# Sparse attention's projections in a two-layer fp32 decoder: seven raw weight buffers instead of three, compressions yielded in four parts, scales and second weights moved to the weights' DMA queue

## The chip, the cores and the metric

One core of one Trainium2 chip runs the whole program, in one launch. The metric is the device time of that launch in microseconds. The core has five engines with their own instruction streams: PE (TensorE, the matrix products), ACT (ScalarE), DVE (VectorE), POOL (GpSimd) and SP (SyncE, which here issues DMAs). They meet by semaphores. An engine executes its stream in order: where one instruction waits, all behind it on that engine wait too.

## The reference

A decoder trunk on x of 1 x 256 x 1024 in fp32, two layers. Layer 0 mixes tokens with native sparse attention (NSA), layer 1 with forgetting attention (FoX); behind each stands an MLP with a squared ReLU.

```python
def reference(x, norm_g, mlp_w_up, mlp_w_down, nsa_w_in, nsa_cmp_pos, nsa_cmp_w1, nsa_cmp_w2, nsa_w_out, ...):
    for i in range(DEPTH):                      # 2
        h = rms_norm(x, norm_g[i, 0])
        m = nsa_mixer(h, ...) if kind == 0 else fox_mixer(h, ...)
        x = x + rms_norm(m, norm_g[i, 1])
        h = rms_norm(x, norm_g[i, 2])
        x = x + rms_norm(squared_relu_mlp(h, mlp_w_up[i], mlp_w_down[i]), norm_g[i, 3])

def nsa_mixer(h, w_in, cmp_pos, cmp_w1, cmp_w2, w_out, cos, sin):
    proj = h @ w_in                             # q, kc, vc, ks, vs, kw, vw, gate
    kcmp = nsa_compress(kc_t, cmp_pos[0], cmp_w1[0], cmp_w2[0])   # silu(windows @ w1) @ w2
    vcmp = nsa_compress(vc_t, cmp_pos[1], cmp_w1[1], cmp_w2[1])
    ...                                         # compressed, selected and windowed branch, gated
    return o.reshape(B, T, H * dh) @ w_out
```

The compression takes 15 overlapping windows of 32 tokens, flattens each (2048 numbers for each of 4 groups), and puts it through a small MLP with 256 hidden units.

## The kernel before, in words

**Products in three.** fp32 operands are split into a rounded part `hi` and the rest `lo`, both in a reduced fp32 type. A product of two fp32 matrices is three products on PE: hi by hi, lo by hi, hi by lo (`mm3`, lines 158 to 160). Tokens stand as two tiles of 128.

**Weights.** Each weight comes in chunks of 128 x 1024 numbers (512 KB). `load_w` (lines 120 to 137) takes a buffer `raw`, issues the DMA from SP (line 131), and splits it: ACT copies `hi` (line 117), DVE subtracts to get `lo` (line 118). A `raw` buffer is free again when its `lo` is done, a `hi`/`lo` pair when PE has used it. The main pool `wpool` has three `raw` and six pairs. Two smaller pools with one `raw` and two pairs each come later: `xpool`, when the evacuation buffers `ev` are closed in the middle of the attention, and `ypool`, when the whole of the attention is done. `load_w` goes round all pools that exist.

**Order of the work.** The string `PLAN` lists the steps of NSA: `c` (blocks that feed the compressions), `v`, `k`, `q` (projection blocks of 256 columns), `p0` and `p1` (the two compressions), and, for the attention, `C`, `S`, `V`, `T` (compressed branch, scores, values, transposes of the output). Each `c`, `v`, `k`, `q`, `p` is a generator; a mention advances it to its next `yield`. `|` closes the compressions' pool; `/` closes `ev` and opens `xpool`. A scheduler then sets each engine's order from dependences and buffers; `keep_in_program_order` pins single instructions to the written order.

**Compression.** `compress` (around lines 428 to 490) builds windows, multiplies them by `w1` in four chunks (line 448) without a `yield` between, adds the halves to `hid` (line 452), transposes it (line 456), applies a sigmoid (line 461) and multiplies by the second weights `w2` (lines 469 and 483). `w2` is loaded by two DMAs of 128 KB from ACT's queue at the start of the program.

**Steps the prediction names.** `q_evac` turns a finished q block into `qr` with rotary embedding (lines 247 to 250), splits it to `qs` and transposes it (line 390) for the scores. `k_evac` and `c_evac` do the like with `kk` (lines 357, 358, 367) and `kd` (lines 336, 344). In the attention, scores are exponentiated on ACT (line 572), transposed on PE (line 585), copied on ACT (`pts`, line 587), and multiplied with the values (line 590); POOL adds the branches (lines 594, 595); PE transposes the result (line 601), and ACT and DVE split it to `aT` (shown as `hT`).

**What follows.** `out_proj` multiplies `aT` by `w_out` in eight chunks p0 to p7 of 128 rows; token tile 0 sums into `ps_m`, tile 1 into `ps_o`, 512 columns each: 96 products. `add_norm` applies the scale g[0][1], `mlp` begins with the scale g[0][2]. Each scale is a 512 KB broadcast load (`load_g`, lines 111 to 114) from ACT's queue.

Of the kernel before, what the change touches and what calls it, by code (L numbers as in the profile page):

```python
# [8 lines left out]
F32 = mybir.dt.float32  # L9
# [4 lines left out]
P = 128  # L14
D = 1024
# [27 lines left out]

PLAN = ("c0 v0 v0 v0 c0 c0 v0 p0 c1 c1 c1 c1 k0 k0 k0 c1 c1 k0 p0 p1 k1 k0 k1 p0 k1 k0 k1 p0 v1 v1 k1 v1 k1 v1 "
# [3 lines left out]
SB_B = 4  # L50
# [6 lines left out]
LEAD = 6  # L57
# [13 lines left out]
def kernel(ctx, tc, x_in, norm_g, w_up, w_down, nsa_w_in, nsa_pos, nsa_w1, nsa_w2,  # L71
                             nsa_w_out, fox_w_in, fox_b_f, fox_w_out, consts, out):
    nc = tc.nc
# [5 lines left out]
    hpool = ctx.enter_context(tc.tile_pool(name="hpool", bufs=2))  # L79
# [6 lines left out]
    def ps_tile(use):  # L86
        return psum.tile([P, 512], F32, name="ps_" + use)
# [20 lines left out]
    cmask = cst[:, C_CMASK:C_CMASK + NT * 16].rearrange("p (t c) -> p t c", t=NT)  # L108
    rowv = cst[:, C_RV:C_RV + NT]
    caus = cst[:, C_CAUS:C_CAUS + P]  # L110
    def load_g(layer, j):
        g = hpool.tile([P, D], F32, name="gb")
        nc.scalar.dma_start(g, norm_g[layer, j:j + 1, :].broadcast_to([P, D]))
        return g

    def split(hi, lo, src):
        act.copy(hi, src)  # L117
        dve.tensor_tensor(out=lo, in0=src, in1=hi.bitcast(F32), op=OP.subtract)  # L118

    def load_w(src, nk, n, later=None):  # L120

        wtiles.append(wtiles.pop(0))
        pool_, nraw = wtiles[-1]

        def view(a):
            return a[:, :nk * n].rearrange("p (k n) -> p k n", k=nk)

        raw = view(pool_.tile([P, 1024], F32, name="raw", bufs=nraw))
        hi = view(pool_.tile([P, 1024], R, name="hi"))
        lo = view(pool_.tile([P, 1024], R, name="lo"))  # L130
        nc.sync.dma_start(raw, src)
        if later is None:
            split(hi, lo, raw)
        else:
            later.append(lambda: act.copy(hi, raw))
            later.append(lambda: dve.tensor_tensor(out=lo, in0=raw, in1=hi.bitcast(F32), op=OP.subtract))
        return hi, lo
# [14 lines left out]
    def queue(ins):  # L152
        if as_traced[0]:
            tc.keep_in_program_order(ins)
# [22 lines left out]
    def new_hT():  # L177

        both = hpool.tile([P, 2, KD, T], R, name="hT")
        return both[:, 0], both[:, 1], both  # L180
# [45 lines left out]
    def tok(hT, k, t):  # L226
        s = slice(t * P, (t + 1) * P)
        return hT[0][:, k, s], hT[1][:, k, s]
# [36 lines left out]
        nc.sync.dma_start(xs[1][:, js], x_in[0, P:T, js])  # L265
    nc.sync.dma_start(cst, consts[:, 0:C_ID])
    hT = new_hT()
    ps = ps_tile("t")
    pe.transpose(ps[:, 0:KD], g8, ident[0:KD, 0:KD])
    dve.tensor_copy(gcol, ps[:, 0:KD])  # L270
# [50 lines left out]
    w2 = cp.tile([P, 2, 2, 2, DH], F32, name="w2")  # L321
    pos_sb = hpool.tile([CLEN // 2, 2, P], F32, name="pos_sb", tag="gb")
    nc.scalar.dma_start(pos_sb, nsa_pos[0].rearrange("j (l two) d -> l j (two d)", two=2))
    for dup in range(2):
        nc.scalar.dma_start(w2[:, :, :, dup, :], nsa_w2[0].rearrange("j (k p) d -> p j k d", p=P))
    ps = ps_tile("t")
    for j in range(2):
        pe.transpose(ps[:, j * 16:(j + 1) * 16], pos_sb[:, j, :], ident[0:16, 0:16])
# [100 lines left out]
    def compress(j):  # L429
# [5 lines left out]
        src = bass.AP(base.tensor, base.offset, [base.ap[0], [2, 16], base.ap[1], [CSTR, NC_]])  # L435
# [7 lines left out]
        for k in range(0, 16, 4):  # L443
            w1 = load_w(wr[:, k:k + 4, :], 4, CH)
            for i in range(4):
                lhs = win2[:, k + i].rearrange("p u c -> p (u c)")
                for u in range(2):
                    queue(pe.matmul(ps[:, 0:CH], lhs, w1[u][:, i, :], start=(k + i + u == 0), stop=(k + i + u == 16)))
        hid = cp.tile([NW, CH], F32, name="hid")
        hs = cp.tile([NW, CH], F32, name="hs")  # L450
        act.copy(hs, ps[64:64 + NW, 0:CH])
# [145 lines left out]
    def attn_T(t, p0, n, on):  # L597

        pt = ps_tile("t")
        for j in range(n):  # L600
            pe.transpose(pt[:, j * P:(j + 1) * P], on[:, 2 * j:2 * j + 2, :].rearrange("p h d -> p (h d)"), ident)
        s = slice(t * P, (t + 1) * P)
        split(aT[0][:, p0:p0 + n, s], aT[1][:, p0:p0 + n, s], pt[:, 0:n * P].rearrange("p (n q) -> p n q", n=n))
# [8 lines left out]
    env, scores, oc, on = {}, {}, {}, {}  # L612
    for cmd in PLAN.split():
        op, arg = cmd[0], cmd[1:]
        if cmd in gens:
            if cmd not in env:
                env[cmd] = gens[cmd]()
            next(env[cmd], None)
            as_traced[0] |= cmd == "c0"
        elif op == ";":  # L620
            as_traced[0] = False
        elif op == "|":
            cmp_ctx.close()
            at = nsa_ctx.enter_context(tc.tile_pool(name="at", bufs=2))
            aT = new_hT()
        elif op == "/":
            ev_ctx.close()
            xpool = ctx.enter_context(tc.tile_pool(name="xpool", bufs=NX_HI, side="right"))
            wtiles += [(xpool, NX_RAW)] * NX_HI
        else:  # L630
            t, p = int(arg[0]), int(arg[1])
            if op == "C":
                oc[t, p] = cmp_attn(t, p)
            elif op == "S":
                scores[t, p] = pair_s(t, p)
            elif op == "V":
                if p % AG == 0:
                    on[t, p // AG] = at.tile([P, 2 * AG, DH], F32, name="on")
                i = 2 * (p % AG)
                pair_v(t, p, scores.pop((t, p)), oc[t, 2 * p // HB], on[t, p // AG][:, i:i + 2, :])  # L640
            elif op == "T":
                attn_T(t, AG * p, AG, on[t, p])
# [43 lines left out]
        finish(rest or ())  # L686
        finish(done(1) or ())

    def out_proj(src, w, layer, after, lead=0):

        g = load_g(layer, 1)
        acc = [lambda c=c: [ps_tile(c) for _ in range(2)] for c in "mo"]
        steps = [(lambda p=p: load_w(w[p * P:(p + 1) * P, :].unsqueeze(1), 1, D), lambda t, p=p: tok(src, p, t))
                 for p in range(KD)]

        def done(t):
            add_norm(t, acc[t], g)
            return after[0](t)

        yield from accumulate(acc, steps, done, lead)  # L700


    def mlp(layer, projection, prepare, after):

        mctx = ExitStack()
        mp = mctx.enter_context(tc.tile_pool(name="mlp", bufs=2))
        g = load_g(layer, 2)
        hT = new_hT()
        qs = []

# [11 lines left out]
        prepare.append(prep)  # L722
        finish(projection)
        g3 = load_g(layer, 3)
        NB = DFF // BW
        us = {}
# [89 lines left out]
        return gen  # L816

    prepare = []
    mlp(0, out_proj(aT, nsa_w_out[0], 0, prepare), prepare, to_fox)


    fox_ctx = ExitStack()
# [2 lines left out]
    hT = fox_in["hT"]  # L825
# [67 lines left out]
    aT = new_hT()  # L893
# [87 lines left out]
            cumsum()  # L981

    prepare = []
    projection = out_proj(aT, fox_w_out[0], 1, prepare, LEAD)

    def fill(n):
        for _ in range(n):
# [15 lines left out]

    fox_ctx.close()

    mlp(1, projection, prepare, None)


# [50 lines left out]
```

## Time and profile before

| | |
|---|---|
| time, median of 3 runs | 677.07 us (673.74 to 677.78) |
| the profiled execution's own time | 679.41 us |
| its span in the profile | 677.6 us |
| PE busy | 655.0 us, 97% of the span |
| ACT busy, DVE busy | 375.3 us (55%), 446.4 us (66%) |
| moved by DMA | 110.17 MB, mean 163 GB/s |
| mean granted clock of PE | 0.99 |

Times in the profile count from the span's start. The projections lie up to about 112 us, with the last compression's end at 83 us; the attention proper runs to about 163 us; `out_proj`'s remaining products to 179.4 us, where the first product of the MLP's `up` starts. "Busy" counts every instruction from start to end; products on PE overlap, so the pitch from start to start is shorter than the duration shown. The page shows 40 equal slices; a table of windows shows the same for stretches that one chooses. Waits are told as "engine, output, line, what released it: total us, times, longest".

### The profile page before, as it was taken

Reading aid. Unit: us, or ns where it says so; the run is one execution under the profiler, and the core shown is the slowest. Engines: PE = TensorE matmul, PEld = TensorE weight load, DVE = VectorE, ACT = ScalarE, POOL = GpSimd, SP = SyncE. Lnnn points to the kernel's source line nnn. Section 1 sums busy time; section 2 is a strip of 40 time slices with the busy share of each in tenths; the row PEclk is TensorE's granted clock in tenths of the full one; section 3 lists DMA queues with packets and bytes.
Section 4 is the critical chain, followed back from the end, with each engine's and each line's share of the span. In section 5 each row is a group of like instructions: output and inputs, shape, how many; then the busy total and the mean of one; then the engine's idle time right before and its main releaser. Section 6 shows DMA issues by size and latency. Waiting matters only on the chain.

```text
span 677.6 us, 10581 instructions
## 1 busy us (share of the span) xinstructions
PE 655.0 (97%) x3993; PEld 571.0 (84%) x3993; DVE 446.4 (66%) x854; ACT 375.3 (55%) x654; POOL 38.5 (6%) x77
## 2 busy tenths in 40 slices
PE   8899999999999999999999989999989999999996
PEld 7888898988888888888889979887878888888884
DVE  4777787754985746566649666774967475566533
ACT  4786677755874545445437655664665345455421
POOL 1000002322100000000005000000100000000000
PEclk9999899999999999999999998999989999999998
DMA  9666743201687646656545853442566566465301
GB/s 308 199 168 202 229 130 124 64 1 34 213 290 218 212 154 215 206 167 211 166 126 148 257 173 108 125 125 64 184 188 194 160 211 211 144 209 184 117 1 62
DMA packets 74802, 110.17 MB, mean 163 GB/s; under 512 B 4696, under 2 KB 60672, under 8 KB 74752
## 3 DMA queue, kind: packets, MB, share of 16 engines
q1 hardware_dynamic: 72336, 105.48, 50.2%
q10 hardware_dynamic: 2416, 4.03, 1.8%
q8 instruction: 31, 0.51, 0.3%
q14 instruction: 19, 0.16, 0.1%
HBM read 108.44 MB, written 1.05 MB: 162 GB/s over the span
## 4 chain that ended last, share of the span: by engine, by line
PE 76%; DMA 9%; DVE 6%; ACT 5%; issue 2%; POOL 1%; SPq 0%; POOLq 0%; DVEq 0%; ACTq 0%
PE ps_m L750 13%; PE ps_m L751 8%; PE ps_o L158 5%; PE ps_o L159 5%; PE ps_o L160 5%; DMA raw<-in_nsa_w_in_dram 5%; PE ps_s L160 5%; PE ps_s L158 5%; PE ps_s L159 5%; PE ps_m L158 4%; PE ps_m L159 4%; PE ps_m L160 4%; PE ps_o L590 3%; ACT hi L117 3%; DVE lo L118 3%; DMA raw<-in_fox_w_in_dram 3%
## 5 line engine op out<-in xcount | busy, mean ns | idle before, releaser
L118 DVE TENSOR_TENSOR lo<-raw,hi 128x1024 fp32r<-128x1024 f32 (+2 forms) x196 | 236.8, 1213 | 127.5 <-ACT hi L117 125.4
L117 ACT CAST hi<-raw 128x1024 fp32r<-128x1024 f32 (+2 forms) x196 | 203.4, 1044 | 144.7 <-DMA raw<-in_mlp_w_up_dram 42.2
L750 PE MATMUL ps_m<-hT,hi 128*128 128x512 f32 x392 | 140.1, 396 | 0.0
L751 PE MATMUL ps_m<-hT,lo 128*128 128x256 f32 x448 | 116.6, 280 | 0.0
L751 PEld LDWEIGHTS ps_m<-hT,lo 128*128 128x128 f32 x448 | 84.5, 189 | 5.0
L750 PEld LDWEIGHTS ps_m<-hT,hi 128*128 128x128 f32 x392 | 73.6, 188 | 16.2
L158 PE MATMUL ps_m<-hi,hT 128*128 128x256 f32 (+3 forms) x236 | 77.1, 327 | 1.9 <-ACT hT L117 1.9
L159 PE MATMUL ps_m<-hi,hT 128*128 128x256 f32 (+3 forms) x236 | 75.9, 321 | 1.6 <-DVE hT L118 1.6
L160 PE MATMUL ps_m<-lo,hT 128*128 128x256 f32 (+3 forms) x236 | 75.4, 320 | 0.0
L160 PE MATMUL ps_s<-lo,uh 128*128 128x512 f32 x128 | 50.5, 395 | 0.0
L159 PE MATMUL ps_o<-hi,ul 128*128 128x512 f32 x128 | 50.5, 395 | 0.0
L158 PE MATMUL ps_s<-hi,uh 128*128 128x512 f32 x128 | 50.5, 395 | 0.0
L158 PE MATMUL ps_o<-hi,uh 128*128 128x512 f32 x128 | 50.5, 395 | 0.0
L159 PE MATMUL ps_s<-hi,ul 128*128 128x512 f32 x128 | 50.5, 394 | 0.0
L160 PE MATMUL ps_o<-lo,uh 128*128 128x512 f32 x128 | 50.4, 394 | 0.0
L158 PEld LDWEIGHTS ps_m<-hi,hT 128*128 128x128 f32 x236 | 45.6, 193 | 5.4 <-ACT hT L117 2.4
L159 PEld LDWEIGHTS ps_m<-hi,hT 128*128 128x128 f32 x236 | 45.7, 194 | 4.6 <-DVE hT L118 2.5
L160 PEld LDWEIGHTS ps_m<-lo,hT 128*128 128x128 f32 x236 | 45.7, 194 | 2.4
L755 ACT COPY second<-ps_m 128x256 f32<-128x256 f32 x56 | 20.8, 371 | 38.7 <-PE ps_m L753 38.7
L158 PE MATMUL ps_m<-hT,hi 128*128 128x256 f32 x128 | 38.5, 301 | 0.0
L159 PE MATMUL ps_m<-hT,lo 128*128 128x256 f32 x128 | 36.5, 286 | 0.0
L160 PE MATMUL ps_m<-hT,hi 128*128 128x256 f32 x128 | 36.5, 285 | 0.0
(242 smaller groups left out, 1119.8 us busy)
## 6 DMA issues: line engine op xcount, KB each, us to landing
raw<-in_mlp_w_up_dram SPq DMA_DIRECT2D x64, 512.0 KB, 3.9
raw<-in_mlp_w_down_dram SPq DMA_DIRECT2D x64, 512.0 KB, 4.2
raw<-in_fox_w_in_dram SPq DMA_DIRECT2D x22, 512.0 KB, 4.6
raw<-in_nsa_w_in_dram SPq DMA_DIRECT2D x18, 512.0 KB, 4.6
raw<-in_nsa_cmp_w_dram SPq DMA_DIRECT2D x8, 512.0 KB, 4.1
raw<-in_nsa_w_out_dram SPq DMA_DIRECT2D x8, 512.0 KB, 4.1
raw<-in_fox_w_out_dram SPq DMA_DIRECT2D x8, 512.0 KB, 3.5
gb<-in_norm_g_dram ACTq DMA_DIRECT2D x7, 512.0 KB, 6.0
```

The lines of the kernel that those rows point to most:

```text
L117: act.copy(hi, src)
L118: dve.tensor_tensor(out=lo, in0=src, in1=hi.bitcast(F32), op=OP.subtract)
L158: queue(pe.matmul(ps, lhs[0], rhs[0], start=start, stop=False))
L159: queue(pe.matmul(ps, lhs[1], rhs[0], start=False, stop=False))
L160: queue(pe.matmul(ps, lhs[0], rhs[1], start=False, stop=stop))
L590: pe.matmul(pov[:, hh, br, :], pts[:, j * P:(j + 1) * P], vt[:, kt, br, g, :], start=(kt == 0), stop=(kt == t))
L750: pe.matmul(psv, wh[:, fs], hT[2][:, :, k, :], start=k == 0, stop=False)
L751: pe.matmul(psv[:, 0, :], wl[:, fs], hT[0][:, k, :], start=False, stop=False)
L755: act.copy(second, psv[:, 1, :])
```

## The change

1. **Seven raw buffers.** A tile `other` of four chunks is put into the second buffer of the pool's `hT` tag, and `load_w` takes its raw buffer in turn from `other` and from `wpool`: four and three, seven in all. At `|`, where the attention takes that buffer for `aT`, the list is set back and `load_w` uses three again.
2. **Compressions in four parts.** `compress` yields after each of the first three chunks of `w1`, and `PLAN` is rewritten up to the first scores: quarters of `p0` and `p1` stand between halves of projection blocks.
3. **Second weights.** The two `w2` loads leave ACT's queue at the start and are pinned on SP's queue behind the first `w1` load.
4. **Scales.** g[0][1] and g[0][2] leave ACT's queue and are issued on SP's, pinned, at `/`; the next weight's DMA is pinned behind them (`behind`). `out_proj` and `mlp` get the scale as an argument.

```diff
-PLAN = ("c0 v0 v0 v0 c0 c0 v0 p0 c1 c1 c1 c1 k0 k0 k0 c1 c1 k0 p0 p1 k1 k0 k1 p0 k1 k0 k1 p0 v1 v1 k1 v1 k1 v1 "
+PLAN = ("c0 v0 v0 v0 c0 c0 v0 p0 c1 c1 c1 c1 p0 k0 k0 p0 k0 c1 c1 k0 p0 k1 k1 p0 p1 k1 k0 k0 k1 v1 p0 v1 p1 k1 v1 "
...
     def load_g(layer, j):
         g = hpool.tile([P, D], F32, name="gb")
-        nc.scalar.dma_start(g, norm_g[layer, j:j + 1, :].broadcast_to([P, D]))
+        src = norm_g[layer, j:j + 1, :].broadcast_to([P, D])
+        if layer == 0 and j < 3:
+            tc.keep_in_program_order(nc.sync.dma_start(g, src))
+            behind[0] = True
+        else:
+            nc.scalar.dma_start(g, src)
         return g
...
+    spare = [None]
+
     def load_w(src, nk, n, later=None):
...
-        raw = view(pool_.tile([P, 1024], F32, name="raw", bufs=nraw))
+        spare.append(spare.pop(0))
+        raw = view(spare[-1] if spare[-1] is not None else pool_.tile([P, 1024], F32, name="raw", bufs=nraw))
         hi = view(pool_.tile([P, 1024], R, name="hi"))
         lo = view(pool_.tile([P, 1024], R, name="lo"))
-        nc.sync.dma_start(raw, src)
+        i = nc.sync.dma_start(raw, src)
+        if behind[0]:
+            tc.keep_in_program_order(i)
+        behind[0] = False
...
     hT = new_hT()
+    other = hpool.tile([P, 4, 1024], F32, name="other", tag="hT")
+    spare[:] = [other[:, 0], None, other[:, 1], None, other[:, 2], None, other[:, 3]]
...
-    for dup in range(2):
-        nc.scalar.dma_start(w2[:, :, :, dup, :], nsa_w2[0].rearrange("j (k p) d -> p j k d", p=P))
...
+            if k == j == 0:
+                for dup in range(2):
+                    tc.keep_in_program_order(
+                        nc.sync.dma_start(w2[:, :, :, dup, :], nsa_w2[0].rearrange("j (k p) d -> p j k d", p=P)))
+                behind[0] = True
+            if k < 12:
+                yield
...
         elif op == "|":
             cmp_ctx.close()
+            spare[:] = [None]
...
         elif op == "/":
             ev_ctx.close()
+            scale01, scale02 = load_g(0, 1), load_g(0, 2)
             xpool = ctx.enter_context(tc.tile_pool(name="xpool", bufs=NX_HI, side="right"))
...
-    mlp(0, out_proj(aT, nsa_w_out[0], 0, prepare), prepare, to_fox)
+    mlp(0, out_proj(aT, nsa_w_out[0], scale01, prepare), scale02, prepare, to_fox)
```

The lines of code shift by up to 20 in the changed kernel: the split is at lines 124 and 125 there, the weights' DMA at 141, the products at 171 to 173, the copies `pts` at 607, the output's transposes at 621.

The order of instructions moves at three places that matter below.

**SP, from the last load of the projections on.** `raw_1245` is the last q chunk. Before, chunks p0 to p5 of `w_out` follow at once (`raw_2085` to `raw_2161`), into `wpool`:

```order
L131 DMA raw_1245<-in_nsa_w_in_dram 128x4x256
L131 DMA raw_2085<-in_nsa_w_out_dram 128x1024
L131 DMA raw_2107<-in_nsa_w_out_dram 128x1024
L131 DMA raw_2125<-in_nsa_w_out_dram 128x1024
L131 DMA raw_2137<-in_nsa_w_out_dram 128x1024
L131 DMA raw_2149<-in_nsa_w_out_dram 128x1024
L131 DMA raw_2161<-in_nsa_w_out_dram 128x1024
L131 DMA raw_2330<-in_mlp_w_up_dram 128x2x512
```

Now the two scales stand there, then p6, p7 and one chunk of `w_up` (`raw_2161`, `raw_2170`, `raw_2512`, all into `xpool`, which has one raw buffer), then p0, p1, p2 (`raw_2073`, `raw_2095`, `raw_2113`), a chunk of `w_up` into `ypool` (`raw_2306`), and only then p3 (`raw_2125`) and the rest:

```order
L141 DMA raw_1233<-in_nsa_w_in_dram 128x4x256
L117 DMA gb_1862<-in_norm_g_dram 128x1024
L117 DMA gb_1864<-in_norm_g_dram 128x1024
L141 DMA raw_2161<-in_nsa_w_out_dram 128x1024
L141 DMA raw_2170<-in_nsa_w_out_dram 128x1024
L141 DMA raw_2512<-in_mlp_w_up_dram 128x4x256
L141 DMA raw_2073<-in_nsa_w_out_dram 128x1024
L141 DMA raw_2095<-in_nsa_w_out_dram 128x1024
L141 DMA raw_2113<-in_nsa_w_out_dram 128x1024
L141 DMA raw_2306<-in_mlp_w_up_dram 128x2x512
L141 DMA raw_2125<-in_nsa_w_out_dram 128x1024
```

The loads of p0 to p5 moved from the end of the projections to behind `xpool`'s loads, and those of p3 to p5 behind a load that needs the attention's end.

**PE, the end of the attention.** `ps_t` from `s_sb` are transposes of scores, `ps_o` from `pts` the products with the values, `ps_t` from `on` the transposes of the output, `ps_m` and `ps_o` from `hi_` products of `w_out`. Before, products of `w_out`'s tile 0 stand among the attention's last steps:

```order
L159 MATMUL ps_m_2091<-hi_2162,hT_1053 128x512
L585 MATMUL ps_t_1978<-ident_74,s_sb_1950 128x128 x4
L160 MATMUL ps_m_2091<-lo_2163,hT_1053 128x512
L590 MATMUL ps_o_1966<-vt_182,pts_1972 128x65 x4
L590 MATMUL ps_o_1966<-vt_182,pts_1983 128x65 x4
L585 MATMUL ps_t_1998<-ident_74,s_sb_1882 128x128 x4
L585 MATMUL ps_t_2009<-ident_74,s_sb_1882 128x128 x4
L158 MATMUL ps_m_2092<-hi_2162,hT_1053 128x512
L590 MATMUL ps_o_1997<-vt_182,pts_2003 128x65 x4
```

Now there are none, and the first one stands behind the last transpose of the output:

```order
L605 MATMUL ps_t_2031<-ident_74,s_sb_1733 128x128 x4
L621 MATMUL ps_t_2049<-ident_74,on_1911 128x128 x2
L610 MATMUL ps_o_2019<-vt_183,pts_2036 128x65 x4
L621 MATMUL ps_t_2054<-ident_74,on_1683 128x128 x2
L621 MATMUL ps_t_2059<-ident_74,on_1988 128x128 x2
L171 MATMUL ps_m_2079<-hi_2074,hT_1041 128x512
L172 MATMUL ps_m_2079<-hi_2074,hT_1041 128x512
L171 MATMUL ps_m_2080<-hi_2074,hT_1041 128x512
```

Of the 96 products of `out_proj`, 35 stood inside the attention before; now all 96 stand behind it. On ACT the casts of p0 to p5 moved along: `hi_2074` (p0) stands right behind the last cast of the attention's output, and on DVE `lo_2075` likewise.

**DVE, the end of the projections.** `hid` is the sum that ends the second compression, `qr` and `rtmp` the rotary embedding of the first q block, `qs` its split, on which PE's transposes at line 390 wait; `lo` rows are splits of weights. Before, `qr` starts ahead of three weights' splits and of `hid`:

```order
L247 TENSOR_TENSOR qr_871<-ps_m_822,rotq_167 128x512
L248 TENSOR_TENSOR rtmp_872<-ps_m_822,rotq_167 128x8x32
L249 TENSOR_TENSOR rtmp_872<-ps_m_822,rotq_167 128x8x32
L118 TENSOR_TENSOR lo_949<-raw_947,hi_948 128x1024
L250 TENSOR_TENSOR qr_871<-qr_871,rtmp_872 128x512
L118 TENSOR_TENSOR lo_1056<-raw_1054,hi_1055 128x1024
L118 TENSOR_TENSOR qs_877<-qr_871,qs_877 128x8x64
L118 TENSOR_TENSOR lo_1062<-raw_1060,hi_1061 128x1024
L452 TENSOR_TENSOR hid_937<-ps_s_880,hs_938 60x256
```

Now it stands behind `hid`, and the sigmoid of the compression stands inside its chain:

```order
L472 TENSOR_TENSOR hid_905<-ps_s_745,hs_906 60x256
L125 TENSOR_TENSOR lo_1229<-raw_1227,hi_1228 128x1024
L260 TENSOR_TENSOR qr_921<-ps_m_841,rotq_168 128x512
L261 TENSOR_TENSOR rtmp_922<-ps_m_841,rotq_168 128x8x32
L262 TENSOR_TENSOR rtmp_922<-ps_m_841,rotq_168 128x8x32
L125 TENSOR_TENSOR lo_1235<-raw_1233,hi_1234 128x1024
L263 TENSOR_TENSOR qr_921<-qr_921,rtmp_922 128x512
L480 TENSOR_SCALAR sg_969<-sg_969 128x120
L481 RECIPROCAL sg_969<-sg_969 128x120
L125 TENSOR_TENSOR qs_927<-qr_921,qs_927 128x8x64
```

The order of `hid` and the first q block changed places on DVE. On PE, the transposes of `hid` now have 36 projection products between the last `w1` product and themselves (24 before), and the transposes of `qs` have 36 products and two short transposes between the q block's last product and themselves (before: 32 products of `w1` and 24 more, with two transposes).

More of the change, by code (lines that the diff above doesn't have):

```diff
@@ L110 @@
     caus = cst[:, C_CAUS:C_CAUS + P]
+    behind = [False]
     def load_g(layer, j):
         g = hpool.tile([P, D], F32, name="gb")
-        nc.scalar.dma_start(g, norm_g[layer, j:j + 1, :].broadcast_to([P, D]))
+        src = norm_g[layer, j:j + 1, :].broadcast_to([P, D])
[4 more added lines that the diff above has]
+            nc.scalar.dma_start(g, src)
         return g
@@ L687, in accumulate, with out_proj @@
         finish(done(1) or ())
-    def out_proj(src, w, layer, after, lead=0):
-        g = load_g(layer, 1)
+    def out_proj(src, w, g, after, lead=0):
         acc = [lambda c=c: [ps_tile(c) for _ in range(2)] for c in "mo"]
@@ L700, in out_proj, with mlp @@
         yield from accumulate(acc, steps, done, lead)
-    def mlp(layer, projection, prepare, after):
+    def mlp(layer, projection, g, prepare, after):
         mctx = ExitStack()
         mp = mctx.enter_context(tc.tile_pool(name="mlp", bufs=2))
-        g = load_g(layer, 2)
         hT = new_hT()
@@ L983 @@
     prepare = []
-    projection = out_proj(aT, fox_w_out[0], 1, prepare, LEAD)
+    projection = out_proj(aT, fox_w_out[0], load_g(1, 1), prepare, LEAD)
     def fill(n):
@@ L1004 @@
     fox_ctx.close()
-    mlp(1, projection, prepare, None)
+    mlp(1, projection, load_g(1, 2), prepare, None)
 _INS = ['x', 'norm_g', 'mlp_w_up', 'mlp_w_down', 'nsa_w_in', 'nsa_cmp_pos', 'nsa_cmp_w1', 'nsa_cmp_w2', 'nsa_w_out',
```

2 rows, old and new, of the table PLAN are left out of this document.

## The prediction

> **What bounds the kernel now.** The profiled execution took 679.41 us for a span of 677.6 us; the median is 677.07 us, 2.3 us less. I make the sum on the profiled execution and take 2.3 us off at the end. I read first the table of windows, cut where the change cuts: start, projections, a stretch at 80 us, the rest of the projections, the attention, `out_proj`'s rest. Columns: window and length, then busy time with counts of PE, its loads, DVE, ACT, POOL, then granted clock, DMA share, GB/s.
>
> ```profile
> 13.00:79.80 66.80, 58.98 (x478) 56.80 (x477) 52.27 (x73) 46.62 (x71) 1.82 (x3) 1.00 0.70 207
> 79.80:83.30 3.50, 3.50 (x21) 3.50 (x20) 2.94 (x4) 2.07 (x4) 0.00 (x0) 0.51 0.82 239
> 83.30:112.00 28.70, 28.07 (x236) 27.14 (x234) 24.56 (x93) 20.87 (x45) 4.01 (x9) 1.00 0.42 136
> 112.00:163.40 51.40, 51.01 (x369) 45.75 (x368) 32.11 (x154) 34.26 (x78) 11.84 (x24) 1.00 0.11 36
> 163.40:179.40 16.00, 15.84 (x77) 12.77 (x77) 12.88 (x22) 12.33 (x23) 2.22 (x5) 1.00 0.54 164
> ```
>
> PE bounds everything. In the projections it lacks 66.80 - 58.98 = 7.8 us; from 83 us on it lacks under 1.2 us in 96. So more raw buffers can win only what PE waits before 83 us. Second, PE's waits there, and what ACT and SP waited for:
>
> ```profile
> PE ps_t L456 <- DVE hid L452: 1.6, 1, 1.6
> PE ps_t L367 <- ACT kk L357: 1.3, 2, 0.7
> PE ps_t L344 <- ACT kd L336: 1.2, 1, 1.2
> PE ps_m L158 <- ACT hT L117: 1.1, 1, 1.1
> PE ps_t L367 <- DVE kk L358: 0.9, 2, 0.5
> PE ps_t L277 <- DVE posT L329: 0.7, 1, 0.7
> PE ps_t L367 <- ACT kT L369: 0.7, 1, 0.7
> PE ps_m L159 <- DVE hT L118: 0.4, 1, 0.4
> ```
> ```profile
> ACT hi L117 <- DMA raw<-in_nsa_w_in_dram: 15.0, 12, 3.3
> ACT hi L117 <- DMA raw<-in_nsa_cmp_w_dram: 2.5, 3, 1.3
> ```
> ```profile
> SPq L131 <- DVE lo L118: 50.9, 24, 4.3
> ```
>
> Not one of PE's waits is for a weight itself: PE waits for evacuations (`kd`, `kk`, `hid`), which stand on ACT and DVE behind splits, and the splits stand behind DMAs that SP issues late, because a raw buffer is free only after `lo`. The waits sum to 7.9 us. To this comes the stretch at half clock, 79.8 to 83.3, right after the longest wait (1.6 us): 3.5 x (1 - 0.51) = 1.7 us. The ceiling of parts 1 and 2 is 9.6 us.
>
> **Raw buffers and quarters of the compressions.** Seven raw buffers let SP run ahead, so the 17.5 us that ACT waited for data go. They cannot all go to the evacuations: six `hi`/`lo` pairs remain, and a cast now stands where PE frees a pair. Wait by wait, with a product of 256 columns at about 0.12 us of PE (58.98 us for 478 instructions):
>
> - start (`hT`, `posT`, 2.2 us): the loads of x and of the first weights come first before and after, only `w2` leaves; I take a quarter off, 0.6 (between 0 and 2.2).
> - `kd`, 1.2: in ACT's order the copy of `kd` stands behind a cast whose pair PE frees only 12 products (1.4 us) ahead of the transposes; cast 1.04 and copy 0.6 us don't fit wholly: 0.9 off.
> - `kk`, 2.2: the first block now has 52 products between its end and its transposes instead of 44, and no DMA holds the casts: 1.6 off.
> - `hid`, 1.6: 36 products of cover instead of 24, all off. `kT`: four transposes' copies now come in one group, 0.4 more.
> - new: `qs`. The first q block now ends 36 products and two transposes before its own transposes, 4.6 us. The chain on DVE, from the trace of before:
>
> ```profile
> 72.56 0.68 DVE L247 TENSOR_TENSOR qr<-ps_m,rotq 128x512 f32<-128x512 f32 x1
> 74.95 0.68 DVE L250 TENSOR_TENSOR qr<-qr,rtmp 128x512 f32<-128x512 f32 x1
> 76.69 0.68 DVE L118 TENSOR_TENSOR qs<-qr,qs 128x512 fp32r<-128x512 f32 x1
> 81.39 0.90 DVE L461 RECIPROCAL sg<-sg 128x120 f32<-128x120 f32 x1
> ```
>
> From `qr`'s start to the end of the second `qr` are 3.1 us (72.56 to 75.63); the sigmoid in between waits for `hid`'s transposes, 24 products (2.9 us) after the block's end, plus ACT's exponential; then reciprocal 0.9 and `qs` 0.68. That ends at 5.4 us, up to 6.3 if the `lo` ahead of `qr` runs over: a wait of 0.8 to 1.7 us. I take 1.3.
>
> Sum: -0.6 - 0.9 - 1.6 - 1.6 + 0.4 + 1.3 = -3.0 us. The half-clock stretch goes if no wait near 1.6 us is left: -1.7 us. Bounds for both together: -9.6, and +1.5 if the evacuations gain nothing from early data and `qs` is added.
>
> **`w2` and the scales.** Rows of the DMA issues before, with the median time to landing last:
>
> ```profile
> gb<-in_norm_g_dram ACTq DMA_DIRECT2D x7, 512.0 KB, 6.0
> w<-in_nsa_cmp_w_dram ACTq DMA_DIRECT2D x2, 128.0 KB, 6.8
> raw<-in_nsa_w_out_dram SPq DMA_DIRECT2D x8, 512.0 KB, 4.1
> ```
>
> `w2` leaves the start, when DMA is nearly full, and lands long before `hid` needs it. The two scales need about 3.5 us of the DMA (1 MB at 300 GB/s, the rate at which 207 GB/s make a share of 0.70), in a stretch where its share is 0.11 to 0.42. By themselves: 0, bounds -0.5 and +0.5. The Trainium skill ("DMA: Bandwidth & Descriptors", "Issuing engines are not separate DMA queues") says that DMAs of all issuing engines run on the same 16 DMA engines; by it, too, the move from ACT's queue to SP's buys no bandwidth, only another order.
>
> That order is what costs. The weight that is pinned behind the scales is p6, for `xpool`, and with it p0 to p5 of `w_out` fall behind `xpool`'s loads.
>
> **The attention loses its filler.** 35 products of `out_proj` stood inside it:
>
> ```profile
> L158 PE MATMUL ps_m<-hi,hT x12: 388/394/480, 115.0 to 157.9; 128*128 128x512 f32 x12
> L159 PE MATMUL ps_m<-hi,hT x12: 389/394/481, 118.2 to 161.0; 128*128 128x512 f32 x12
> L160 PE MATMUL ps_m<-lo,hT x11: 387/396/481, 118.4 to 155.0; 128*128 128x512 f32 x11
> ```
>
> Their pitch is read from the timeline of what follows (start, duration):
>
> ```profile
> 163.39 0.61 PE L601 MATMUL ps_t<-ident,on 128*128 128x128 f32 x4
> 165.63 0.33 PE L601 MATMUL ps_t<-ident,on 128*128 128x128 f32 x1 [0.16 <-POOL on L595]
> 167.41 0.39 PE L160 MATMUL ps_m<-lo,hT 128*128 128x512 f32 x1
> 170.12 0.39 PE L160 MATMUL ps_m<-lo,hT 128*128 128x512 f32 x1
> 175.80 1.03 PE L191 MATMUL ps_t<-ident,h 128*128 128x128 f32 x8
> 179.41 0.39 PE L158 MATMUL ps_m<-hi,hT 128*128 128x512 f32 x1
> ```
>
> 13 products start from 167.41 to 170.12: 0.226 us each, so 35 are 7.9 us. How much shorter does the attention get without them? All 7.9 if PE's own work bounds it, nothing if they stood in waits. One place where they stand thick:
>
> ```profile
> 120.94 0.39 PE L158 MATMUL ps_m<-hi,hT 128*128 128x512 f32 x1
> 123.24 0.40 PE L160 MATMUL ps_m<-lo,hT 128*128 128x512 f32 x1
> 123.47 0.38 PE L540 MATMUL ps_t<-ident,pc 128*128 128x128 f32 x2
> ```
> ```profile
> 122.50 0.30 ACT L537 ACTIVATE pc<-sc 128x120 f32<-128x120 f32 x1
> ```
>
> Nine products fill 2.0 us up to the transposes of `pc`, but `pc` is ready only at 122.80: here 0.7 of 2.0 us come back. Later they stand singly between transposes and value products, where PE has other work. I take half over all: -4.0 us, ends 0 and -7.9.
>
> **`out_proj` behind the attention.** Before, 16.0 us pass from 163.39 to the first product of `up` (179.41), with 61 products of `out_proj` and both groups of transposes. How long the output's last cast and a weight's split take:
>
> ```profile
> 166.35 0.36 ACT L117 CAST hT<-ps_t 128x256 fp32r<-128x256 f32 x1
> ```
> ```profile
> L118 DVE TENSOR_TENSOR lo<-raw,hi 128x1024 fp32r<-128x1024 f32 (+2 forms) x196 | 236.8, 1213 | 127.5 <-ACT hi L117 125.4
> L117 ACT CAST hi<-raw 128x1024 fp32r<-128x1024 f32 (+2 forms) x196 | 203.4, 1044 | 144.7 <-DMA raw<-in_mlp_w_up_dram 42.2
> ```
>
> Before, that cast stood behind a weight's; now it starts when the transposes at 165.63 (0.33) are done, at 166.0, and ends at 166.35. Then comes `hi` of p0, and only then a product: PE starts at 167.4. 96 x 0.226 = 21.7 us, the eight transposes 0.8 in the pipeline: `up` starts at 189.9, 26.5 us after 163.39: +10.5 us. Each further chunk costs DVE 1.21 us and PE 12 x 0.226 = 2.7, so the splits keep ahead. p3 is loaded only when p0's `lo` has freed a raw buffer, at about 168.6; 4.1 us to landing and 1.04 to its cast make 173.8, and PE has 30 products of p0 to p2, until 174.2: just in time, up to +1.5 us if not. PE stands still from 163.9 (four transposes after 163.39) to 167.4 but for one pair of transposes: I take one stretch of half clock there, as at 79.8: +1.7 us. Bounds of this part: +9 and +13.7.
>
> The Trainium skill ("TensorE: Matmul & The Clock Gate", "What's actually happening") says that the clock falls after a whole idle window of about 3.4 us. The trace doesn't agree: 0.51 was granted after a wait of 1.6 us. By the page the stretch broken by transposes would not throttle, and the sum would be 1.7 us lower, 678.9 us.
>
> The MLPs and FoX keep their order but for a few rows that change places: 0.
>
> **The sum.** -3.0 - 1.7 + 0 - 4.0 + 10.5 + 1.7 = +3.5 us: 682.9 us for an execution like the profiled one, 680.6 us against the median.
>
> **Rivals.**
>
> *Faster (0.18).* The attention is bound by PE's own work, since PE is busy 51.01 of 51.40 us there, and gives all 7.9 back; the projections give their ceiling, 9.6; the tail costs 10.5 without half clock. Sum -7.0: 670.1 us. For it: early data free ACT and DVE at all evacuations at once. Against: `pc` above, and casts that now wait for six pairs. With two thirds of both gains it is -1.2, inside my forecast.
>
> *Slower (0.17).* For the attention's chain stands this row of its waits (112 to 180 us):
>
> ```profile
> ACT pts L587 <- PE ps_t L585: 8.7, 9, 2.1
> ```
>
> ACT waits for PE's transposes, and PE's value products wait for ACT's copies: a chain that runs in both directions, in whose holes the scheduler put the 35 products. If they stood in holes only, the attention gives nothing, and holes laid open to 1.6 us and more halve the clock once more, 1.7 us. Sum 3.5 + 4.0 + 1.7 = +9.2: 686.3 us. It passes 1% once the attention gives under 2.5 us with that half clock, or under 0.8 without. Against: PE is busy for 51.01 of 51.40 us there, and 35 products seldom fit so many holes exactly.
>
> *The raw buffers do nothing (0.13).* ACT's wait for DMA turns into an equal wait for PE's pairs; the evacuations stay as late as before, and the clock still falls at the compression's end. The projections give 0 to +1.5 instead of -4.7: +8.2 to +9.7, 685.3 to 686.8 us. For it: a pair is freed only by PE. Against: the 50.9 us that SP waited for `lo`.
>
> **Chances.** The forecast has 0.52, the rivals 0.18, 0.17 and 0.13. About 1%, 6.8 us, is what a measurement of this kernel can tell from no change: 670.3 to 683.8 us. The forecast lies within, the first rival just beyond one end, the other two beyond the other: faster 0.18, same 0.52, slower 0.30. The range, 670 to 687 us, goes from the first rival's time to the other two's, so that about half of the first and a third of the others fall outside it. Time: 680.6 us.
>
> **What would show it.** Projections: ACT's `hi` no longer waits for `in_nsa_w_in`, but for PE; PE's waits for `kd`, `kk`, `hid` fall from 5.0 to about 0.9 us; one of about 1.3 us appears at `qs`; no half clock at 80 us. Attention: no `out_proj` product in it, about 4 us shorter. Tail: from the four transposes of the output to `up` about 26.5 us, PE's first product waiting for `hi` of p0. The forecast is wrong if the attention shortens by over 6 us or by under 2, or if p0's split is found to be done earlier.

## The result, and the profile after

| | before | after |
|---|---|---|
| median | 676.88 us (673.74 to 677.78, 4 runs) | 685.9 us (684.66 to 687.29, 4 runs) |
| ratio, with its 95% interval | | 1.0142 (1.0104 to 1.018) |
| the profiled execution | 679.41 us, span 677.6 us | 687.29 us, span 685.4 us |

The change makes the kernel slower, by 1.4%: 9.0 us between the medians, 7.8 us between the two profiled spans (before's profiled execution lies 2.5 us above its median, after's 1.4 us).

The windows of after, cut at the places that answer to those of before; columns as there:

```profile
13.00:79.80 66.80, 61.45 (x487) 59.42 (x485) 54.86 (x77) 47.96 (x73) 2.77 (x4) 0.97 0.70 209
79.80:83.30 3.50, 2.96 (x26) 2.85 (x27) 1.32 (x4) 1.18 (x2) 0.00 (x0) 1.00 0.02 5
83.30:112.00 28.70, 27.34 (x223) 26.42 (x223) 18.47 (x88) 16.13 (x42) 3.88 (x10) 0.97 0.06 19
112.00:163.90 51.90, 46.05 (x330) 39.53 (x329) 30.95 (x150) 32.82 (x74) 10.89 (x24) 0.98 0.14 52
163.90:168.40 4.50, 1.36 (x8) 0.90 (x8) 2.05 (x6) 2.25 (x4) 0.91 (x2) 1.00 0.18 51
168.40:171.80 3.40, 3.40 (x9) 2.64 (x9) 3.40 (x4) 2.38 (x3) 0.00 (x0) 0.50 0.68 230
171.80:192.30 20.50, 20.50 (x95) 16.96 (x95) 15.36 (x20) 13.48 (x22) 1.12 (x2) 1.00 0.77 252
```

Two things are to be seen. The attention (fourth row) is as long as before, 51.90 us for 51.40, but PE is now busy for only 46.05 us in it. And behind it come a hole (1.36 of 4.50 us busy), a stretch at half clock, and 20.5 us of pure products, where before had 16.0 us in all.

Where each stage ends is read from the first and last start of two groups, the transposes of `qs` (the last ends the projections) and of the attention's output `on` (the last ends the attention). Of before, then of after:

```profile
L390 PE MATMUL ps_t<-ident_r,qs x32: 223/248/332, 79.6 to 109.0; 128*128 128x128 f32 x32
...
L601 PE MATMUL ps_t<-ident,on x16: 270/272/328, 112.6 to 165.6; 128*128 128x128 f32 x16
```
```profile
L403 PE MATMUL ps_t<-ident_r,qs x32: 223/248/280, 80.2 to 107.4; 128*128 128x128 f32 x32
...
L621 PE MATMUL ps_t<-ident,on x16: 270/273/421, 111.2 to 166.2; 128*128 128x128 f32 x16
```

The projections end 1.6 us earlier; the attention takes 58.8 us from there instead of 56.6 (+2.2). The tail, from the timeline of after:

```profile
166.15 0.33 PE L621 MATMUL ps_t<-ident,on 128*128 128x128 f32 x1 [1.73 <-POOL on L615]
167.89 0.50 PE L171 MATMUL ps_m<-hi,hT 128*128 128x512 f32 x1 [1.41 <-ACT hi L124]
...
192.32 0.39 PE L171 MATMUL ps_m<-hi,hT 128*128 128x512 f32 x1
```

From the output's last transposes to `up`'s first product are 26.2 us, where before had 13.8 (165.63 to 179.41): +12.4. What follows takes 493.1 instead of 498.2 us (span less the start of `up`): -5.1. Together -1.6 + 2.2 + 12.4 - 5.1 = +7.9, the difference of the spans within rounding.

No run ties the last term to the change. Two stretches of before, at the start of FoX and near its end, ran at half clock; after has none there:

```profile
407.40:410.90 3.50, 3.50 (x19) 3.50 (x18) 2.31 (x12) 2.40 (x10) 0.00 (x0) 0.51 0.47 150
496.20:499.60 3.40, 3.40 (x11) 2.74 (x11) 1.80 (x3) 2.05 (x3) 0.00 (x0) 0.50 0.56 182
```

They cost 1.7 us each. The other 1.8 us is idle time of PE, above all one wait for `qk_hi`: 2.2 us in before, ahead of the first of these stretches, and at most 0.9 in any other trace. Kernels below that have the same FoX show none, one or both of these stretches. In the stages that the change touches, the two profiled executions thus differ by +13.0 us; FoX brings that to +7.9.

Last, PE's longest waits in after, from 8 to 120 us:

```profile
PE ps_t L403 <- DVE qs L125: 1.5, 1, 1.5
PE ps_m L172 <- DVE hT L125: 1.2, 1, 1.2
PE ps_t L380 <- ACT kT L382: 1.1, 1, 1.1
PE ps_s L586 <- DVE mx L589: 1.1, 1, 1.1
PE ps_t L292 <- DVE posT L342: 0.8, 1, 0.8
PE ps_m L171 <- ACT hT L124: 0.7, 1, 0.7
```

The waits for `kd`, `kk` and `hid` are gone (two for the transposed `hid`, 0.5 us together, stand below this list); `qs` is new, and those of the start (`hT`, `posT`) are 2.7 us, 0.5 more than before.

### The profile page after: what moved, and what is told of

Same layout as the page of the kernel before. It is cut to its first block, busy times and chain, and to the rows that moved or that the text cites. A ratio compares the mean times of both kernels' runs of the same rounds, so it can differ in the third digit from the quotient of the medians.

```text
span 685.4 us, 10578 instructions
## 1 busy us (share of the span) xinstructions
PE 657.4 (96%) x3993; PEld 571.0 (83%) x3993; DVE 447.2 (65%) x854; ACT 375.3 (55%) x654; POOL 38.0 (6%) x77
## 4 chain that ended last, share of the span: by engine, by line
PE 76%; DVE 7%; DMA 6%; ACT 6%; issue 3%; POOL 1%; SPq 0%; POOLq 0%; DVEq 0%; ACTq 0%
PE ps_m L770 13%; PE ps_m L771 8%; PE ps_o L171 5%; PE ps_o L172 5%; PE ps_o L173 5%; PE ps_s L173 5%; PE ps_s L171 5%; PE ps_s L172 5%; PE ps_m L171 4%; PE ps_m L172 4%; PE ps_m L173 4%; PE ps_o L610 3%; DVE lo L125 3%; ACT hi L124 3%; DMA raw<-in_mlp_w_up_dram 2%
## 5 line engine op out<-in xcount | busy, mean ns | idle before, releaser
L125 DVE TENSOR_TENSOR lo<-raw,hi 128x1024 fp32r<-128x1024 f32 (+1 forms) x183 | 221.5, 1216 | 121.4 <-ACT hi L124 119.3
L124 ACT CAST hi<-raw 128x1024 fp32r<-128x1024 f32 (+1 forms) x183 | 189.9, 1046 | 125.2 <-DMA raw<-in_mlp_w_up_dram 42.3
```

## The experiments

Each comparison below is with the kernel before, run on the same chip in the same turn; its medians there were 676.62 us (e1 to e4), 677.05 us (e5 to e8) and 676.94 us (e9 to e11). The runs are called e1 to e11: the pin taken out is e1, the scales alone e2, the raw buffers alone e3, the quarters with the raw buffers e4, the raw buffers with `w2` e5, to that the scales e6, the same without raw buffers e7, the exchange in `PLAN` e8, and the last three kernels e9 to e11. Theory A of the expectations: the pin that puts the next weight behind the scales makes the loss. Theory B, its rival: the new order of the projections costs in itself.

### The pin alone taken out of the changed kernel

```diff
         if layer == 0 and j < 3:
             tc.keep_in_program_order(nc.sync.dma_start(g, src))
-            behind[0] = True
         else:
```

> The changed kernel with one line less: the weight behind the two scales is not pinned to them. By the order of instructions p0 to p5 of w_out stand ahead of the scales again, and 39 of the 96 out_proj products stand ahead of the attention's last transpose (0 in the changed kernel, 40 before). Theory A (the pin makes the whole loss): attention and tail go back to before's lengths, 14.5 us less than the changed kernel in those two (2.1 + 12.4), and the time comes to 671 to 677 us, depending on whether the 5 us that the changed kernel wins in FoX stay. Theory B (the new order of the projections costs in itself): the time stays above 680 us.

Measured: 679.64 us (675.32 to 683.56), ratio to before 1.0043 (1.0014 to 1.0071). Its profile (span 675.8 us):

```profile
L402 PE MATMUL ps_t<-ident_r,qs x32: 224/248/282, 78.7 to 107.0; 128*128 128x128 f32 x32
...
L620 PE MATMUL ps_t<-ident,on x16: 270/272/421, 110.7 to 167.4; 128*128 128x128 f32 x16
```
```profile
167.36 0.33 PE L620 MATMUL ps_t<-ident,on 128*128 128x128 f32 x1 [0.17 <-POOL on L614]
...
181.37 0.39 PE L170 MATMUL ps_m<-hi,hT 128*128 128x512 f32 x1
```

One line took the tail from 26.2 back to 14.0 us. The attention is 60.3 us here with its 39 products, and 58.8 without them in the changed kernel (both have one stretch of half clock at its start): the 35 to 39 products, 8 to 9 us of PE, give back 1.6 us. What they leave behind is holes: from the last `qs` to the last `on` PE waits 2.2 us in e1 and 8.9 us in the changed kernel. In the medians the pin costs 6.3 us (the profiled execution of e1 lies below its median, that of the changed kernel above: between those two it is 9.5). But the kernel stays 3 us above before, outside what theory A allowed: neither theory has it all.

### The scales' part alone on the kernel before

```diff
+        src = norm_g[layer, j:j + 1, :].broadcast_to([P, D])
+        if layer == 0 and j < 3:
+            tc.keep_in_program_order(nc.sync.dma_start(g, src))
+            behind[0] = True
...
             ev_ctx.close()
+            scale01, scale02 = load_g(0, 1), load_g(0, 2)
```

> The kernel before with the scales' part alone (part 4): three raw buffers, the old PLAN. No out_proj product stands in the attention. Theory A: attention 0 to 2 us longer in spite of 35 products less, tail about 12 us longer: 686 us if the 5 us of FoX come along with it, 691 us if they don't. Theory B: under 680 us.

Measured: 689.99 us (689.61 to 692.87), ratio 1.0203 (1.0169 to 1.0237), 13.4 us more than before. Here, too, PE waits through the attention (107 to 167 us), above, where before waited 0.3 us from 112 to 163.4 us, below (1.1 us from its last `qs` to its last `on`):

```profile
PE ps_s L577 <- DVE mx L580: 3.3, 4, 1.2
PE ps_o L601 <- ACT pts L598: 2.1, 7, 0.5
PE ps_s L577 <- DVE w L529: 0.7, 1, 0.7
PE ps_t L551 <- ACT pc L548: 0.6, 2, 0.3
```
```profile
PE ps_t L540 <- ACT pc L537: 0.3, 1, 0.3
```

With the old order of the projections, the same holes open where the products stood: 58.8 us from the last `qs` to the last `on` against 56.6, one stretch of half clock included. The tail is 26.2 us (171.3 to 197.5), as in the changed kernel. The time lies within theory A's 686 to 691 us; theory B as the whole of it is out.

### Seven raw buffers alone

```diff
+        spare.append(spare.pop(0))
+        raw = view(spare[-1] if spare[-1] is not None else pool_.tile([P, 1024], F32, name="raw", bufs=nraw))
...
+    other = hpool.tile([P, 4, 1024], F32, name="other", tag="hT")
+    spare[:] = [other[:, 0], None, other[:, 1], None, other[:, 2], None, other[:, 3]]
```

> The kernel before with seven raw buffers alone (part 1); compressions and PLAN as before. If early data alone shorten the waits for kd, kk and hid, the projections end 2 to 4 us earlier: 673 to 675 us. If casts only wait for PE's pairs instead, nothing: 676 to 678 us.

Measured: 674.43 us (671.28 to 676.84), ratio 0.9964 (0.9941 to 0.9987): a small gain, at the edge of what was expected. Its profile shows one large wait of PE and where it comes from:

```profile
PE ps_m L161 <- ACT hT L117: 4.0, 1, 4.0
```
```profile
18.23 1.04 ACT L117 CAST hi<-other 128x1024 fp32r<-128x1024 f32 x1 [6.09 <-DMA other<-in_nsa_w_in_dram]
...
19.80 1.12 ACT L117 CAST hT<-h 128x512 fp32r<-128x512 f32 x2
```

ACT waits 6.1 us for a weight to land, and the cast of the activations `hT`, which PE needs, stands behind it. DMA is full there (share 1.07 to 1.09 from 6 to 24 us). More loads are in flight, and they land later: of the weights issued in the first 16 us, those into `raw` took 7.7 us to land (median) and those into `other` 10.0; before it was 7.3. Before, the cast at this place started at 15.03 us. The buffers that were to take waits away have made one, at the start.

### Raw buffers and second weights; then the scales unpinned; then those without the raw buffers

The kernel above, with `w2` behind the first `w1` load (compressions whole):

```diff
-    for dup in range(2):
-        nc.scalar.dma_start(w2[:, :, :, dup, :], nsa_w2[0].rearrange("j (k p) d -> p j k d", p=P))
...
+            if k == j == 0:
+                for dup in range(2):
+                    tc.keep_in_program_order(
+                        nc.sync.dma_start(w2[:, :, :, dup, :], nsa_w2[0].rearrange("j (k p) d -> p j k d", p=P)))
+                behind[0] = True
```

> The kernel before with seven raw buffers and the second weights behind the first w1 load (parts 1 and 3); old PLAN, compressions whole, scales as before. Theory C: with seven raw buffers alone, too many loads share the DMA at the start, the second weight's cast waits 6.1 us, the hT of token tile 1 stands behind it on ACT, and PE waits 4.0 us at 16.2 us; two stretches of half clock follow. The w2 loads, issued on ACT's queue at the start, are part of the crowd and hold SP's loads of x back (issued 4.5 to 8.2 us; 2.7 to 4.0 in the changed kernel). Without them the wait falls below 2.5 us and the time to 669 to 673 us. Rival: the seven weights alone make the crowd; the wait stays near 4 us and the time near 674.4 us.

Measured: 671.52 us (669.71 to 675.1), ratio 0.9926 (0.9892 to 0.9959): faster than both kernels. SP's loads of x's second tile leave earlier, and PE's wait for `hT` falls from 4.0 to 1.4 us. The issues of x in e3, then here, and the wait:

```profile
4.53 3.64 SPq L268 DMA_DIRECT2D x<-in_x_dram  x2
```
```profile
3.78 1.30 SPq L273 DMA_DIRECT2D x<-in_x_dram  x2
```
```profile
PE ps_m L166 <- ACT hT L119: 1.4, 1, 1.4
```

So theory C holds in the wait and the time: with `w2` on ACT's queue, SP's loads of x leave late. The other traces agree: with `w2` there, before issues the second of them at 7.5 us; without it, the changed kernel issues it at 3.7 us. `w2` is 256 KB, but also some thousand small packets (1254 of under 512 bytes in the first 16 us of e3, 205 here); which of the two holds SP back is not separated.

To that, the scales on SP's queue at the opening of `xpool`, without the pin:

> As the one before, and the scales on SP at the opening of xpool, without the pin of the next weight (parts 1, 3 and 4 without the pin, old PLAN). Before, a scale's load of 512 KB is issued from ACT's queue at about 12 us (a first one at 5 us): 1 MB less at the start. Theory C: another 1 to 3 us less, 667 to 671 us, the best of all. Rival: the scales at the start are hidden; the same as without them within 1 us.

Measured: 673.73 us (672.49 to 679.53), ratio 0.995 (0.9929 to 0.9971). Not 1 to 3 us less than without the scales, but 2.2 more: theory C fails here, and so does its rival. In the profiles, from the last `qs` to the last `on`, e6 takes 60.0 us (106.5 to 166.5) and e5 56.8; a stretch of half clock is 1.7 of the 3.2. These two profiled executions lie far from their medians (e6's is the slowest of its 11 runs, e5's the fastest of 8), but the other traces place the cost there, too. From the last `qs` to the last `on`, with 1.7 us taken off for a stretch of half clock, the four kernels with the scales on SP's queue and no pin (e1, e6, e7, e8) take 58.3 to 59.5 us, the seven with the scales on ACT's (before, e3, e4, e5, e9, e10, e11) 55.9 to 56.8. So the scales' move makes the attention about 2 us longer. Why was not settled: in e7 PE waits only 0.6 us more there than in e5.

The same without the raw buffers:

> Parts 3 and 4 without the pin, and nothing else: three raw buffers, old PLAN. If the start's crowd costs before as well (PE waits 2.2 us for hT and posT there), 1 to 2 us less than before: 674.5 to 676 us. If it is only the seven raw buffers that make it a crowd: 676 to 678 us.

Measured: 675.01 us (672.47 to 677.62), ratio 0.9973 (0.9952 to 0.9994): -2.0 us. The start's crowd costs with three raw buffers, too: PE's waits for `hT` and `posT`, 2.2 us before, are 1.2 us here.

### Quarters of the compressions: where the rest of the loss lies

The changed kernel without parts 3 and 4:

> The changed kernel without parts 3 and 4: seven raw buffers, compressions in quarters, new PLAN; second weights and scales on ACT's queue as before. Theory A: about the time of the unpinned kernel within 1.5 us, 671 to 677 us. If the moves of w2 and scales to SP matter by themselves, the two differ by more.

Measured: 681.67 us (679.03 to 686.4), ratio 1.0081 (1.0043 to 1.0119). Outside what theory A expected, and 7.2 us above raw buffers alone. e1 stands 5.9 us above e6 (6.3 with each taken against before in its own turn) by the same difference, part 2. The prediction's new wait, at `qs`, was a first suspect:

```diff
-        "p1 k1 v1 p0 q0 p1 q0 q0 p1 q0 q1 q1 p1 q1 q0 q0 q1 p1 | q2 q2 S00 q2 q1 q1 S01 q2 ; C00 S02 V00 q3 q3 q3 q3 q2 q2 V01 S03 "
+        "p1 k1 v1 p0 q0 p1 q0 q0 p1 q0 q1 q1 p1 q1 q1 q0 q0 p1 | q2 q2 S00 q2 q1 q1 S01 q2 ; C00 S02 V00 q3 q3 q3 q3 q2 q2 V01 S03 "
```

> The unpinned kernel with two steps of PLAN exchanged: 12 more projection products stand ahead of the transposes of the first qs (48 and two transposes instead of 36). The prediction's term: the wait at qs measured 1.5 to 2.3 us in three runs with the new PLAN; 12 products are 1.4 us, so it falls to under 0.9 us. With it the risk of a stretch of half clock behind it falls: 675 to 678 us instead of 679.6. If qs is put off by as much on DVE: no change.

Measured: 679.09 us (673.71 to 680.28), ratio 1.0017 (0.999 to 1.0043), above the 675 to 678 us that were expected, and 0.5 us less than e1, which is no difference. The wait fell from 2.1 to 1.0 us, nearly as forecast; it was not the 6 us.

Then three kernels that put the two halves of the new `PLAN` on e5 one by one, ahead of the bar (quarters) and behind it (the attention's first steps):

> The kernel of parts 1 and 3 (671.5 us) with the changed kernel's PLAN behind the bar alone (the last q blocks and first scores); compressions whole. Open is where the 6 to 7 us lie by which the kernels with part 2 are slower than those without (679.6 to 673.7, 681.7 to 674.4). Theory D (the quarters' order ahead of the bar costs it: qs wait, kk wait, half clock behind them): no change, 670.5 to 673 us. Theory E (the order behind the bar, which starts the attention, costs it): 675 to 678 us.

> Parts 1, 2 and 3 with the changed kernel's PLAN ahead of the bar (quarters of the compressions) and the old one behind it. Theory D: 676 to 680 us, the wait at qs 1.5 to 2.3 us. Theory E: 670.5 to 673 us.

> Parts 1, 2 and 3, the scales as before: the changed kernel's whole PLAN. The fourth corner of the two above: 676 to 679 us by either theory, about 6 us above parts 1 and 3 alone. If it is near 671.5 us, part 2 costs only together with something else.

Measured, against e5's 671.52: behind the bar alone 672.17 us (ratio to before 0.9934, 0.991 to 0.9958); ahead of it alone 677.7 (1.0017, 0.998 to 1.0054); both 680.98 (1.006, 1.0029 to 1.009). Theory D holds: the order ahead of the bar costs 6.2 us, the other nothing by itself. On top of the first it adds about 3 more, which puts the fourth corner above its 676 to 679 us; that step is at the edge of what the runs can tell (674.51 to 684.18 us for e10, 676.7 to 683.5 for e11), and its cause was not looked for. PE's three longest waits in e10, 8 to 112 us:

```profile
PE ps_t L352 <- ACT kd L344: 3.0, 1, 3.0
PE ps_t L398 <- DVE qs L120: 2.0, 1, 2.0
PE ps_t L375 <- ACT kT L377: 1.1, 1, 1.1
```

In e5 the first is 0.4 us and the second isn't there. The copy that makes `kd` stands on ACT behind a `w1` quarter's cast and two more weights', which wait for landings (18 to 24 us: DMA share 1.13):

```profile
22.02 1.05 ACT L119 CAST hi<-other 128x1024 fp32r<-128x1024 f32 x1 [0.24 <-DMA other<-in_nsa_cmp_w_dram]
24.63 1.04 ACT L119 CAST hi<-raw 128x1024 fp32r<-128x1024 f32 x1 [1.56 <-DMA raw<-in_nsa_w_in_dram]
26.08 1.04 ACT L119 CAST hi<-other 128x1024 fp32r<-128x1024 f32 x1 [0.41 <-DMA other<-in_nsa_w_in_dram]
27.03 0.61 ACT L344 COPY kd<-kd 128x512 f32<-128x512 f32 x1
```

It ends at 27.64 us, in e5 at 26.86, where three casts stand ahead of it as well. So only 0.8 us of the 3.0 is a later copy; the rest is that e5's PE came to it later, after a longer wait for `hT` (1.7 us for 0.7) and a half-clock stretch of its own from 17.6 us on. By the stage's end e10 is 5.1 us behind e5 (last `qs` at 109.9 and 104.8). Shown is that the order ahead of the bar costs this; the wait at `qs` is 2.0 of it, and how the rest divides among the other waits and the half-clock stretches is not separated.

The steps in the medians, one on top of the other, each kernel taken against before in its own turn: raw buffers -2.2, `w2` -3.3, scales without the pin +2.2, quarters with their `PLAN` +6.3, the pin +6.0. Their sum is +9.0 us, by which the changed kernel lies above before. The two gains are little more than a third of the three losses. Each step holds for this order of steps: on the kernel before, scales and pin together cost 13.4 us (e2), here 8.2.

## Why the prediction was right, and where not

The time lies in the stated range, 670 to 687 us, but 5.3 us above the 680.6, and over 1% above before, where the forecast had 0.30. By the profiled executions it is in part luck that it lies in the range: in the stages that the change touches they differ by +13.0 us where the sum has +3.5, and 5.1 us in FoX, on which the sum says 0, make up for half of the gap. Step by step, in the profiled executions:

- **One cause of the loss**, the pin, was placed right; the quarters, which cost as much in the medians, were not seen. The scales' pin moves `w_out`'s loads, all 96 products stand behind the attention, and one line less brings them back (e1).
- **The tail** was forecast at +10.5 + 1.7 = +12.2 us; it measured +12.4, half clock included (0.50 from 168.40 to 171.80).
- **The attention** is the step that failed: "I take half over all: -4.0 us". Measured +2.2, of which 1.7 are a half-clock stretch: against before there was no shortening (+0.5), against the kernel that differs by the pin alone it was 1.6 us. By the prediction's own sign (a shortening of under 2 us) its account of the attention is wrong. The scales' move, for which the sum has 0, makes the attention about 2 us longer in the kernels without the pin; less the 1.6 us, that is near the +0.5. The products had stood in holes: PE's waits in the attention went from 0.3 to 5.9 us. The prediction held against this that PE was busy for 51.01 of 51.40 us; but a stage whose holes are filled looks busy, too. The holes are those of the rival that ends slower (686.3 us). Its other half is not shown: the half clock of the attention starts at 110.37 us, where no `out_proj` product had stood (the first at 115.0 before), and e1, which has the products, has it as well. The place at 121 us, 0.7 given back of 2.0, was nearer to the truth than the half, which I had taken for the places "where PE has other work".

PE's waits in the attention of after, 112 to 163.9 us:

```profile
PE ps_o L610 <- ACT pts L607: 2.6, 8, 0.5
PE ps_s L586 <- DVE mx L589: 2.3, 3, 1.2
PE ps_s L586 <- DVE w L538: 0.7, 1, 0.7
PE ps_t L560 <- ACT pc L557: 0.3, 1, 0.3
```

- **The projections** were to give 4.7 us and gave 1.6. The raw buffers did what was said: ACT's waits for `in_nsa_w_in` (10 to 80 us) fell from 15.0 to 4.5 us, and only 3.7 us of waits for PE's products came in their place, so the rival by which the buffers do nothing (685.3 to 686.8 us) is out, though its time fits. `kd`, `kk` and `hid` went as said (4.5 of 5.0 us, with the 0.5 of the transposed `hid` counted, where 4.1 were forecast), `kT` rose by 0.4 as said, `qs` came with 1.5 us (1.3 forecast). The start failed: 0.5 us more instead of 0.6 less. And the half clock did not go, it moved, from 79.8 to 18.2 us, behind the start's wait: the step "the half-clock stretch goes if no wait near 1.6 us is left" missed that two waits close together do the same.
- **Parts 3 and 4 "by themselves: 0, bounds -0.5 and +0.5"** was too narrow on both sides: `w2` gives about 3 us (e3 to e5), the scales cost 2.2 (e5 to e6). For `w2` the step that failed is the price of a load at the start: I counted DMA time, not what its issue holds back on SP and whose cast stands behind on ACT. For the scales it stays open why the attention gets longer.
- **The quarters** stand in the sum with gains (at `kk` and `hid`) and with 0.4 and 1.3 us of new waits (`kT`, `qs`). In the medians they cost about 6 us: the order ahead of the bar does it (e10), and how that divides among waits and half clock is open.

## What to carry to other kernels

A product that a scheduler has put into the holes of a chain costs little there (here 1.6 of 8 to 9 us) and its full length where PE is the limit: before moving what feeds it, ask where it will stand, and don't credit the chain with its time. A pinned order on a DMA queue pins everything that a pool's turn hangs on it: here one line put six loads behind a pool that opens late. And buffers that let loads run ahead are worth what the queue's start can bear: the gain went from 2.2 to 5.5 us when two small loads had left the start.

## What was not expected of the hardware

The granted clock halves for fixed stretches. The trace's own record of the clock in after has them here (start in us from the span's start, length, granted share):

```
18.21   3.41   0.5
110.37  3.41   0.5
168.40  3.41   0.5
```

The distances are 92.16 and 58.03 us, 27 and 17 times 3.413. In twelve of the thirteen traces of this study the stretches lie on such a grid (e7 has none before the program's last microseconds), and what stands ahead of most of them is a stretch of the same length in which PE was busy for about half or less. Of before, then of after (window and length, then PE's busy time first and the granted clock near the end):

```profile
76.39:79.80 3.41, 1.79 (x16) 1.52 (x15) 2.53 (x4) 2.30 (x3) 0.00 (x0) 1.00 0.89 246
79.80:83.21 3.41, 3.41 (x20) 3.41 (x20) 2.85 (x4) 2.07 (x4) 0.00 (x0) 0.50 0.83 240
```
```profile
14.80:18.21 3.41, 1.73 (x13) 1.33 (x11) 3.41 (x5) 3.41 (x8) 0.19 (x1) 1.00 1.00 276
18.21:21.62 3.41, 3.25 (x15) 3.25 (x16) 2.64 (x7) 2.82 (x4) 1.36 (x2) 0.50 0.88 227
106.96:110.37 3.41, 2.34 (x21) 2.10 (x19) 2.37 (x18) 2.78 (x8) 1.72 (x4) 1.00 0.42 142
110.37:113.78 3.41, 3.12 (x11) 2.60 (x11) 1.03 (x6) 1.91 (x7) 0.31 (x1) 0.50 0.03 12
164.99:168.40 3.41, 0.84 (x3) 0.61 (x4) 1.33 (x4) 1.88 (x3) 0.91 (x2) 1.00 0.23 68
168.40:171.81 3.41, 3.41 (x9) 2.65 (x9) 3.41 (x4) 2.38 (x3) 0.00 (x0) 0.50 0.69 230
```

Counted over these twelve traces, up to 660 us and over stretches that ran at full clock themselves: 21 stretches of the grid had PE busy for under 0.56 of their length, and 20 of them were followed by half clock; of the other 2263, 13 were. Nine of these lie where the attention begins, with products of 32 columns, like the middle pair of after (2.34 of 3.41 us busy). Three stretches at half clock were followed by a second one, with PE busy for 0.73 to 1.00 of the first. So a stretch about half busy is nearly always enough, but it is not the whole condition. And one wait can halve the clock or not, by where it falls on a grid that the program doesn't set: behind waits for `qs` of 2.0 to 2.2 us half clock followed in e4 and e11, not in e10, where the wait lies across two stretches of the grid, and not in e1, the one exception of the 21. The times of one kernel spread with it: the unpinned kernel's runs went from 675.32 us at a mean granted clock of 0.999 to 683.56 at 0.982. The Trainium skill ("TensorE: Matmul & The Clock Gate", "What's actually happening") has the free-running window of about 3.4 us, and the traces agree with its length and that it runs free; it asks for an idle window, where the traces show that a window half busy is enough.
